# Weights 64 bytes (modulo 512) from their moving operands; the second FFN in 256-column matmuls; three output pieces summed on TensorE

## The chip, the core and the metric

One core of a Trainium2 chip runs the whole program. The time is device microseconds (us) of one execution; the kernel before has a median of 2463.41 us over three runs (2462.46 to 2465.11). Engines are named as in the profile: PE is TensorE's matmul side, PEld its weight loads, DVE VectorE, ACT ScalarE, POOL GpSimd, SP the engine that issues most DMAs.

## What is computed

Two layers of a decoder trunk over 256 positions of width 2048, in float32. Each layer adds three sub-layers to the residual stream: a token mixing (one input projection, three head groups, one output projection), a cross-attention into 256 memory tokens, and a SwiGLU FFN with 5632 hidden columns.

```python
def swiglu(h, w_gu, w_down):
    gu = jnp.einsum('bsd,dcf->bscf', h, w_gu)
    return jnp.einsum('bsf,fd->bsd', jax.nn.silu(gu[:, :, 0]) * gu[:, :, 1], w_down)

h = x
for l in range(DEPTH):                      # 2
    ...                                     # mixing and cross-attention, each h = h + rms_norm(.., g)
    ff = swiglu(rms_norm(h, f_pre_g[l]), f_w_gu[l], f_w_down[l])
    h = h + rms_norm(ff, f_post_g[l])
return h
```

## The kernel before

**The split.** A float32 product is made of three matmuls of the rounded type float32r. Each weight block (`raw`, 1 MB, loaded by SP) is split into `hi` (ACT, L208) and `lo` (DVE, L209), 1024 columns at a time, in rings of three buffers (pool `ws`). Activations exist as two halves too: `x` (normalised residual, transposed; made by `new_x`, L549), `mh`/`ml` (memory), `cqh`/`cql`, `kvn` (latents), `mxx` and `m6` (mixing result), `cx` (cross-attention result), `hx` (FFN hidden). All matmuls are recorded at the line of the helper `mm`, L203, so they are told apart by tiles: in `acc<-x,hi` the result is `acc`, and `x` and `hi` are the two operands. Each matmul has a weight load of its own (128 columns, 512 bytes of each partition), which PEld does beside the matmul ahead of it.

**Three forms of a projection.** `mm_t` (L394) puts the weights of the network into the array and moves `x`: for each 128x128 block three matmuls of 256 columns, lo by xh, hi by xh, hi by xl. `mm_w` (L413) does the same block with two: hi by both halves of `x` side by side (512 columns) and lo by xh (256 columns); the two halves of the result are added behind by `add_up` (L424: per tile one ACT copy and one DVE add out of PSUM). `mm_n` (L431) puts the activations into the array and moves hi, lo, hi, 256 to 512 columns each.

**Which form where.** Mixing, cross-attention queries and keys use `mm_t`; values and all output projections (`project_out`, L668) use `mm_n`. In both FFNs the first two steps of the up-projection (`hf == 0 and j < 4`) use `mm_t` and the other twenty use `mm_w`, two calls each: 40 calls of 16 blocks by 2, that is 1280 pairs of a 512- and a 256-column matmul in each layer. `plan` (L264) lists the weight blocks in the same order: for `mm_t` in the FFN one block of gate and up columns side by side (`pairs`, two DMAs of 512 KB per `raw`), for `mm_w` one 1 MB DMA.

**Addresses.** Pools lay tiles out one behind the other. `new_x` allocates 72 spare words and starts `x` `off` bytes ahead of them; `off` is 32 for mixing and cross-attention, 256 and 128 for the two FFNs. `pa` and `pc` hold 32 bytes each and shift what lies behind them. The distance used below is the address of the weights less that of the moving operand in the same partition, modulo 512 bytes, worked out from the places that the pools give the tiles. The strides of both are multiples of 512 bytes (but for the 336-column block of `ckv`), so a stage has one distance.

**Between stages.** After an output projection, `residual` (L611) adds the normalised result to `H` in pieces, and `turn_x` transposes and splits each into the next `x`; the first matmuls of the next stage follow piece by piece (the ramp). In two places `warm` (L444) gives PE 38 filler matmuls. Helper work of the attention runs as generators, advanced by `pump` once per weight block. At the end `last_residual` (L709) forms the statistics, then scales and adds eight pieces of 128x512: six on DVE (L721), two by ACT (scale, L718) and POOL (add, L719), each followed by its DMA out. A scheduler orders each engine's queue; in the ramps the order of DVE and ACT is that of the code.

## Time and profile before

| what | value |
|---|---|
| median of three runs | 2463.41 us |
| the profiled execution | 2460.3 us |
| its span, first to last instruction | 2458.6 us |
| PE busy | 2419.2 us, 98% |
| DVE, ACT, POOL busy | 59%, 50%, 12% |
| up-projection of the first FFN | about 484 to 737 and 859 to 1105 us |
| up-projection of the second FFN | about 1700 to 1955 and 2076 to 2323 us |

A matmul's recorded duration includes its pipeline, so neighbours overlap; what a matmul costs is the distance from its start to the next one's start. That is read from two rows of the timeline with the number of matmuls between them, from a piece of the chain of waits (`x168` is its count), or from a stretch that holds one form alone.

### The profile page before, as it was taken

How to read it: one execution, taken by the hardware profiler on the slowest of the kernel's cores; microseconds unless marked ns; L12 is line 12 of the kernel's file. 1: busy time of each engine (PE TensorE's matmuls, PEld its weight loads, DVE VectorE, ACT ScalarE, POOL GpSimd, SP SyncE). 2: the span in 40 equal slices, each digit the busy share in tenths (PEclk: the TensorE clock that was granted, in tenths of full speed). 3: DMA queues.
4: the chain of work that ended last, by engine and by line, in shares of the span. 5: the costliest groups of instructions: out<-in, count | busy, mean ns of one | idle time of the engine just before them, and what ended most of it. 6: DMA issues, size and time to landing. Idle time of an engine off the chain costs nothing.

```text
span 2458.6 us, 37634 instructions
## 1 busy us (share of the span) xinstructions
PE 2419.2 (98%) x15169; PEld 2170.7 (88%) x15169; DVE 1456.6 (59%) x2249; ACT 1240.9 (50%) x1936; POOL 296.8 (12%) x228
## 2 busy tenths in 40 slices
PE   9999999999999999999999999999999999999997
PEld 8899789998888988888999987998988889888887
DVE  5676767665554455555466767676555544555554
ACT  5655545564444444444455555465544444444443
POOL 0010131011110011111110102111111100111101
PEclk9999999999999999999999999999999999999999
DMA  7755575455555555555554555644555555555553
GB/s 247 238 168 155 165 259 176 154 172 188 188 189 191 186 193 188 188 186 197 180 171 131 190 147 194 206 171 150 181 188 187 188 195 189 186 187 187 188 194 129
DMA packets 362371, 452.95 MB, mean 184 GB/s; under 512 B 8730, under 2 KB 281044, under 8 KB 361684
## 3 DMA queue, kind: packets, MB, share of 16 engines
q1 hardware_dynamic: 360756, 443.97, 54.9%
q0 software_dynamic: 1248, 6.29, 0.8%
q8 instruction: 119, 1.95, 0.3%
q14 instruction: 56, 0.46, 0.1%
q10 hardware_dynamic: 192, 0.28, 0.0%
HBM read 444.72 MB, written 5.79 MB: 183 GB/s over the span
## 4 chain that ended last, share of the span: by engine, by line
PE 93%; DVE 3%; DMA 1%; ACT 1%; issue 0%; SPq 0%; DVEq 0%; ACTq 0%
PE acc L203 89%; DVE lo L209 1%; PE ixp L203 1%; PE xtp L595 1%; PE lga L203 0%; DVE mx L209 0%; ACT hi L208 0%; DVE H L624 0%; DMA H<-in_x_dram 0%; PE warm L448 0%; PE pva L203 0%; DMA m<-in_mem_dram 0%; PE pvb L203 0%; PE lgx L203 0%; PE pvx L203 0%
## 5 line engine op out<-in xcount | busy, mean ns | idle before, releaser
L209 DVE TENSOR_TENSOR lo<-raw,hi 128x1024 fp32r<-128x1024 f32 (+2 forms) x839 | 1012.9, 1208 | 813.5 <-ACT hi L208 812.4
L208 ACT ACTIVATE hi<-raw 128x1024 fp32r<-128x1024 f32 (+2 forms) x839 | 859.4, 1025 | 897.4 <-PE acc L203 812.9
L203 PE MATMUL acc<-x,hi 128*128 128x512 f32 (+2 forms) x4800 | 1298.7, 342 | 0.0
L203 PE MATMUL acc<-x,lo 128*128 128x256 f32 x3680 | 990.7, 282 | 7.9 <-ACT x L214 4.5
L203 PEld LDWEIGHTS acc<-x,hi 128*128 128x128 f32 (+1 forms) x4800 | 818.6, 188 | 107.7 <-issue 2.0
L203 PEld LDWEIGHTS acc<-x,lo 128*128 128x128 f32 x3680 | 691.6, 188 | 23.0 <-ACT x L214 9.7
L203 PE MATMUL acc<-hi,hx 128*128 128x512 f32 (+1 forms) x1760 | 452.6, 347 | 0.0
L203 PEld LDWEIGHTS acc<-hi,hx 128*128 128x128 f32 x1760 | 308.6, 189 | 41.7
L203 PE MATMUL acc<-lo,hx 128*128 128x512 f32 (+1 forms) x880 | 304.5, 347 | 0.0
L203 PEld LDWEIGHTS acc<-lo,hx 128*128 128x128 f32 x880 | 166.7, 189 | 20.3
L1272 POOL TENSOR_TENSOR u<-u,rbh 128x512 f32<-128x512 f32 x40 | 51.9, 1297 | 1004.0 <-DVE u L429 1004.0
L203 PE MATMUL acc<-hi,mx 128*128 128x512 f32 (+1 forms) x576 | 149.7, 347 | 7.1 <-ACT mx L208 5.3
L203 PEld LDWEIGHTS acc<-hi,mx 128*128 128x128 f32 x576 | 100.7, 191 | 21.3 <-ACT mx L208 6.3
L203 PE MATMUL acc<-hi,x 128*128 128x384 f32 (+1 forms) x384 | 110.0, 362 | 0.0
L1247 POOL TENSOR_TENSOR g<-g,u 128x512 f32<-128x512 f32 x44 | 92.6, 2104 | 72.0 <-ACT g L1257 68.9
L203 PE MATMUL acc<-lo,mx 128*128 128x512 f32 (+1 forms) x288 | 99.3, 345 | 0.0
L203 PEld LDWEIGHTS acc<-hi,x 128*128 128x128 f32 x384 | 70.0, 188 | 7.5 <-issue 2.0
L203 PE MATMUL acc<-lo,x 128*128 128x384 f32 (+1 forms) x192 | 69.3, 361 | 0.0
L214 ACT ACTIVATE x<-xtp,gT 128x256 fp32r<-128x256 f32 x96 | 40.2, 471 | 45.3 <-PE xtp L595 45.3
L427 ACT ACTIVATE g<-acc 128x256 f32<-128x256 f32 x80 | 30.5, 381 | 60.1 <-PE acc L203 60.1
L203 PEld LDWEIGHTS acc<-lo,mx 128*128 128x128 f32 x288 | 55.0, 191 | 6.2
L427 ACT ACTIVATE u<-acc 128x256 f32<-128x256 f32 x80 | 30.4, 379 | 58.5 <-PE acc L203 58.5
(250 smaller groups left out, 2053.2 us busy)
## 6 DMA issues: line engine op xcount, KB each, us to landing
raw<-in_f_w_gu_dram SPq DMA_DIRECT2D x160, 1024.0 KB, 5.0
raw<-in_f_w_down_dram SPq DMA_DIRECT2D x76, 1024.0 KB, 5.0
raw<-in_w_out_dram SPq DMA_DIRECT2D x30, 1024.0 KB, 5.3
raw<-in_w_in_dram SPq DMA_DIRECT2D x48, 512.0 KB, 4.8
raw<-in_w_in_dram SPq DMA_DIRECT2D x23, 1024.0 KB, 5.6
raw<-in_x_wkv_dram SPq DMA_DIRECT2D x16, 1024.0 KB, 4.9
raw<-in_f_w_gu_dram SPq DMA_DIRECT2D x32, 512.0 KB, 4.5
raw<-in_w_in_dram SPq DMA_DIRECT2D x12, 960.0 KB, 5.2
```

Source lines behind the costliest of these rows:

```text
L203: return nc.tensor.matmul(o, lhsT=lhsT, rhs=rhs, start=start, stop=stop, skip_group_check=True)
L208: nc.scalar.activation(hi, src, AF.Copy)
L209: eng.tensor_tensor(lo, src, hi.bitcast(F32), op=ALU.subtract)
L214: nc.scalar.activation(hi, src, AF.Copy, scale=scale)
L427: nc.scalar.activation(dst[:, b, :], t[:, 256:512], AF.Copy)
L595: nc.tensor.transpose(p[:, t * P:(t + 1) * P], src[:, t, (c + j) * P:(c + j + 1) * P], ident)
L1247: nc.gpsimd.tensor_tensor(g, g, u, op=ALU.mult)
L1272: nc.gpsimd.tensor_tensor(u, u, two(fnx["rb"]), op=ALU.mult)
```

## The change

**Distances.** `pa` is gone, `new_x` has 16 spare words, all `off` are 64, gaps of 384 bytes are put at the start of the pools `mp` and `kp`, and `cx` starts 128 bytes later. What results (bytes modulo 512; counts over both layers):

| moving operand, weights | columns, count | before | after |
|---|---|---|---|
| x, hi/lo: mixing, cross queries | 256, 2448 | 32 | 64 |
| x, hi/lo: odd blocks of ckv | 256, 144 | 352 | 384 |
| cqh/cql/kvn, hi/lo: latents | 256, 408 | 448 | 64 |
| mh/ml, hi/lo: memory keys | 256, 384 | 448 | 64 |
| hi/lo, mh/ml: memory values | 256, 384 | 64 | 448 |
| hi/lo, x: values of A, gating | 384, 384 and 512, 192 | 480 | 448 |
| hi/lo, kvn: values of B | 384, 48 | 64 | 448 |
| hi/lo, m6: part of the first piece of w_out | 512, 48 in each layer | 64; 192 | 448; 64 |
| hi/lo, mx and hx: w_out, f_w_down | 256 and 512 | 0 | 0 |
| hi/lo, cx: x_wo | 512, 144 and 256, 96 | 64 | 64 |
| x, hi/lo: first FFN, first two steps | 256, 384 | 256 | 64 |
| x, hi/lo: first FFN, the rest | 512 and 256, 1280 pairs | 256 | 64 |
| x, hi/lo: second FFN, first two steps | 256, 384 | 128 | 64 |
| x, hi/lo: second FFN, the rest | 1280 pairs, after: 3840 of 256 | 128 | 64 |

**Form.** In the second layer (`l` is 1) every step of the up-projection uses `mm_t` and `act` in place of `mm_w` and `act_w`, and `plan` loads its blocks as `pairs`.

**End.** In `last_residual` three of the eight pieces are summed in PSUM: PE adds `ident` by H, and, once the statistics are there, `dg` (the row factors on a diagonal, from `spread`) by `og`; ACT copies the sum out and issues its DMA. The other five stay on DVE. POOL has no part in it.

```diff
-    pa = ctx.enter_context(tc.tile_pool(name="pa", bufs=1))
-    nc.gpsimd.memset(pa.tile([P, 8], F32, name="half_pa"), 0.0)
...
-                    if hf == 0 and j < 4:
-                        yield spec(pairs(a["f_w_gu"][l], j * P, 256), KD, 512)
+                    if l or hf == 0 and j < 4:
+                        yield spec(pairs(a["f_w_gu"][l], (hf * nh + j) * P, 256), KD, 512)
...
-        x = xp.tile([P, f + 72], F32R, tag="xx", name=nm)[:, 72 - off // 4:72 - off // 4 + f]
+        x = xp.tile([P, f + 16], F32R, tag="xx", name=nm)[:, 16 - off // 4:16 - off // 4 + f]
...
+        pieces = [(t, slice(g * 512, (g + 1) * 512)) for g in range(4) for t in range(2)]
+        summed = {}
+        for t, f in pieces[:3]:
+            summed[t, f.start] = p = acc.tile([P, 512], F32, tag="acc", name="hsum")
+            mm(p, ident, H[:, t, f], True, False)
+        dg = spread(r)
         rest()
-        for t in range(2):
-            for c0, n, beside in ((512, 512, True), (0, 512, False), (1024, 512, False), (1536, 512, False)):
-                f = slice(c0, c0 + n)
-                if beside:
-                    nc.scalar.activation(og[:, t, f], og[:, t, f], AF.Copy, scale=r[:, t:t + 1])
-                    nc.gpsimd.tensor_tensor(H[:, t, f], H[:, t, f], og[:, t, f], op=ALU.add)
-                else:
-                    nc.vector.scalar_tensor_tensor(H[:, t, f], og[:, t, f], r[:, t:t + 1], H[:, t, f],
-                                                   op0=ALU.mult, op1=ALU.add)
-                (nc.scalar if t and beside else nc.sync).dma_start(out[0, t * P:(t + 1) * P, f], H[:, t, f])
+        for t, f in pieces[:3]:
+            mm(summed[t, f.start], dg[:, t, :], og[:, t, f], False, True)
+        for i in (3, 0, 4, 1, 5, 2, 6, 7):
+            t, f = pieces[i]
+            p = summed.get((t, f.start))
+            if p is not None:
+                nc.scalar.activation(H[:, t, f], p, AF.Copy)
+            else:
+                nc.vector.scalar_tensor_tensor(H[:, t, f], og[:, t, f], r[:, t:t + 1], H[:, t, f],
+                                               op0=ALU.mult, op1=ALU.add)
+            (nc.sync if p is None else nc.scalar).dma_start(out[0, t * P:(t + 1) * P, f], H[:, t, f])
...
-        res["x"] = xh, xl, _ = new_x("x", 32)
+        res["x"] = xh, xl, _ = new_x("x", 64)
...
+        nc.gpsimd.memset(mp.tile([P, 96], F32, name="gap"), 0.0)
...
+            nc.gpsimd.memset(kp.tile([P, 96], F32, name="gap"), 0.0)
...
-        begin(residual(og, oss, evac, ("x_pre_g", l), nx, False, 32), 2, -1)
+        begin(residual(og, oss, evac, ("x_pre_g", l), nx, False, 64), 2, -1)
...
-        cx = kp.tile([P, 2, 4, 256], F32R, name="cx")
+        cx = kp.tile([P, 2080], F32R, name="cx")[:, 32:].rearrange("p (a h t) -> p a h t", a=2, h=4)
...
-        begin(residual(og, oss, evac, ("f_pre_g", l), nx, True, (256, 128)[l]), 3, 0)
+        begin(residual(og, oss, evac, ("f_pre_g", l), nx, True, 64), 3, 0)
...
-                if hf == 0 and j < 4:
+                if l or hf == 0 and j < 4:
...
-            begin(residual(og, oss, evac, ("mix_pre_g", l + 1), cur, True, 32), 3, 0)
+            begin(residual(og, oss, evac, ("mix_pre_g", l + 1), cur, True, 64), 3, 0)
```

The queue of PE where the second half of the second FFN's up-projection starts, behind the last matmul of the down-projection, before (the number behind a name tells one tile from another; two `acc` tiles hold two blocks of 128 gate columns):

```order
L203 MATMUL acc_19895<-hi_19980,hx_16862 128x256
L203 MATMUL acc_20061<-x_16817,hi_20010 128x512
L203 MATMUL acc_20062<-x_16817,hi_20010 128x512
L203 MATMUL acc_20061<-x_16817,lo_20011 128x256
L203 MATMUL acc_20062<-x_16817,lo_20011 128x256
```

and with the change (the two tiles hold two blocks of gate and two of up columns):

```order
L201 MATMUL acc_20590<-x_16820,lo_20539 128x256
L201 MATMUL acc_20590<-x_16820,hi_20538 128x256
...
L201 MATMUL acc_20591<-x_16820,lo_20539 128x256
L201 MATMUL acc_20591<-x_16820,hi_20538 128x256
...
L201 MATMUL acc_20590<-x_16820,hi_20538 128x256 x2
L201 MATMUL acc_20591<-x_16820,hi_20538 128x256 x2
```

Two matmuls per block of weights became three, each of 256 columns and each with a weight load; outside this up-projection and the end PE's, DVE's and ACT's queues hold the same operations in the same order as before.

The queue of PE from the start of the last piece of the last output projection (132 matmuls, of which the middle is left out), before:

```order
L203 MATMUL acc<-hi,hx 128x256 [waits Activation_49]
L203 MATMUL acc<-hi,hx 128x256
L203 MATMUL acc<-lo,hx 128x256 [waits DVE_49]
...
L203 MATMUL acc<-hi,hx 128x256
L1318 UNCONDITIONAL_BRANCH
```

and with the change:

```order
L201 MATMUL acc<-hi,hx 128x256 [waits Activation_49]
L201 MATMUL acc<-hi,hx 128x256
L201 MATMUL hsum<-H,ident 128x512 [waits DVE_49]
L201 MATMUL acc<-lo,hx 128x256 [waits DVE_49]
...
L201 MATMUL acc<-hi,hx 128x256
L201 MATMUL hsum<-H,ident 128x512
L201 MATMUL hsum<-H,ident 128x512 [waits DVE_49]
L201 MATMUL hsum<-og,dg 128x512 [waits DVE_49,Pool_49]
L201 MATMUL hsum<-og,dg 128x512 [waits Pool_49]
L201 MATMUL hsum<-og,dg 128x512 [waits Activation_49]
```

One of the three sums of `H` stands ahead of the last piece's matmuls and waits for DVE to empty an `acc` tile of the piece before (L686 in the kernel before); the other two stand behind the last piece, and the three of `og` at the end.

The end of ACT's queue, before:

```order
L582 ACTIVATE sqj,sso<-og 128x256 [waits DVE_49,Activation_49] x2
L718 ACTIVATE og<-og,rs_r 128x512 [waits DVE_49,Pool_49]
L718 ACTIVATE og<-og,rs_r 128x512 [waits Pool_49]
L723 DMA out_dram<-H 128x512 [waits Pool_49]
L1318 UNCONDITIONAL_BRANCH
```

and with the change:

```order
L580 ACTIVATE sqj,sso<-og 128x256 [waits DVE_49,Activation_49] x2
L518 ACTIVATE dg<-ident,rs_r 128x128 [waits DVE_49]
L724 ACTIVATE H<-hsum 128x512 [waits PE_49]
L728 DMA out_dram<-H 128x512 [waits Activation_49]
L724 ACTIVATE H<-hsum 128x512 [waits PE_49] x2
L728 DMA out_dram<-H 128x512 [waits Activation_49] x2
L1325 UNCONDITIONAL_BRANCH
```

ACT now waits for PE where it scaled for POOL, and issues three DMAs where it issued one.

## Rows read from the trace of the kernel before

**Rows 1.** Page, part 1: busy time, share of the span, instructions.
```profile
PE 2419.2 (98%) x15169; PEld 2170.7 (88%) x15169; DVE 1456.6 (59%) x2249; ACT 1240.9 (50%) x1936; POOL 296.8 (12%) x228
```
**Rows 2.** Waits of PE: who for whom, total us, times, longest.
```profile
PE acc L203 <- DVE lo L209: 5.8, 8, 1.2
PE acc L203 <- ACT mx L208: 5.3, 4, 2.0
```
**Rows 3.** Stretches, PE alone: us, length, PE busy (matmuls), granted clock, DMA share, GB/s.
```profile
826.90:858.60 31.70, 31.70 (x266) 1.00 0.60 192
858.60:1104.80 246.20, 246.20 (x1410) 1.00 0.57 188
2076.00:2323.00 247.00, 247.00 (x1410) 1.00 0.57 188
```
**Rows 4.** Timeline of PE, cross-attention's output projection: start us, us, instruction.
```profile
458.72 0.40 PE L203 MATMUL acc<-lo,cx 128*128 128x512 f32 x1
...
472.02 0.39 PE L203 MATMUL acc<-hi,cx 128*128 128x512 f32 x1
472.38 0.28 PE L203 MATMUL acc<-lo,cx 128*128 128x256 f32 x1
...
477.59 0.28 PE L203 MATMUL acc<-hi,cx 128*128 128x256 f32 x1
```
**Rows 5.** Timeline of PE: latents at 82 us, cross-attention's queries at 411 us.
```profile
82.58 0.28 PE L203 MATMUL acc<-cqh,lo 128*128 128x256 f32 x1
...
85.40 0.28 PE L203 MATMUL acc<-cqh,lo 128*128 128x256 f32 x1
...
411.09 0.28 PE L203 MATMUL acc<-x,lo 128*128 128x256 f32 x1
...
423.99 0.28 PE L203 MATMUL acc<-x,hi 128*128 128x256 f32 x1
```
**Rows 6.** Chain of waits: start us, us, what; cross logits, then both FFNs' first steps.
```profile
430.44 0.86 PE lgx L203 x4
506.57 17.27 PE acc L203 x144
1723.63 17.08 PE acc L203 x144
```
**Rows 7.** Stretches: length, PE, PEld, DVE, ACT, POOL busy, granted clock, DMA, GB/s.
```profile
158.00:240.00 82.00, 81.71 (x633) 76.58 (x631) 55.01 (x140) 47.54 (x107) 4.64 (x5) 1.00 0.55 171
378.00:402.00 24.00, 22.79 (x195) 22.61 (x194) 22.58 (x40) 19.34 (x41) 6.96 (x4) 1.00 0.41 145
2445.00:2459.00 14.00, 0.00 (x0) 0.00 (x0) 8.53 (x19) 2.22 (x6) 4.83 (x4) 0.62 0.41 150
```
**Rows 8.** Groups of the second FFN (1742 to 2445 us): busy us, mean ns, idle before.
```profile
L209 DVE TENSOR_TENSOR lo<-raw,hi 128x1024 fp32r<-128x1024 f32 x248 | 308.1, 1242 | 290.2 <-ACT hi L208 290.2
L429 DVE TENSOR_TENSOR g<-acc,g 128x256 f32<-128x256 f32 x40 | 16.9, 421 | 13.6 <-ACT g L427 13.6
L1289 ACT ACTIVATE og<-acc 128x512 f32<-128x512 f32 x6 | 3.5, 588 | 2.9 <-PE acc L203 2.9
L1256 DVE TENSOR_TENSOR g<-acc,rbh 128x512 f32<-128x512 f32 x2 | 1.4, 688 | 0.2 <-PE acc L203 0.2
```
**Rows 9.** DMA issues: count, KB of each, median us to landing.
```profile
raw<-in_f_w_gu_dram SPq DMA_DIRECT2D x32, 512.0 KB, 4.5
```
**Rows 10.** Timeline of DVE at the last output piece and at the end.
```profile
2428.50 0.42 DVE L686 TENSOR_TENSOR og<-acc,og 128x256 f32<-128x256 f32 x1 [1.64 <-PE acc L203]
...
2448.43 0.16 DVE L505 SCALAR_TENSOR_TENSOR rs_r<-rs_u,rs_r 128x2 f32<-128x2 f32 x1
2448.71 6.08 DVE L721 SCALAR_TENSOR_TENSOR H<-og,rs_r,H 128x512 f32<-128x512 f32 x6
```
**Rows 11.** Single lines and tiles: count, ns min/median/max, first and last start.
```profile
L721 DVE SCALAR_TENSOR_TENSOR H<-og,rs_r,H x6: 740/749/1751, 2448.7 to 2454.0; 128x512 f32<-128x512 f32 x6
L519 DVE TENSOR_SCALAR dg<-ident,rs_r x10: 279/287/289, 27.1 to 1737.7; 128x128 f32<-128x128 f32 x10
```

## The prediction

> **What bounds the kernel now.** I read the page first: PE is busy for 98% of the span [rows 1]. Then the waits of PE: the longest sums are 5.8 and 5.3 us [rows 2], so nearly all of the 2460.3 us of the profiled execution is the spacing of matmuls. The question is what a matmul costs, and the rows to look at are starts, not durations. Granted clock is 1.00 (2.4 GHz) in the stretches used.
>
> Spacing of 256-column matmuls, by distance of weights from moving operand: at 0 bytes 31.70 us / 264 = 120.1 ns (the 266 of the row hold two that reach in from the side) [rows 3]; at 64, (477.59 - 472.38) / 46 = 113.3 ns, and 512 columns beside it (472.02 - 458.72) / 57 = 233.3 ns [rows 4]; at 448, (85.40 - 82.58) / 24 = 117.5; at 32, (423.99 - 411.09) / 109 = 118.3 [rows 5]; at 256, 17.27 / 144 = 119.9, and at 128, 17.08 / 144 = 118.6 [rows 6]. A pair of `mm_w` (512 and 256 columns) takes 246.20 / 704 = 349.7 ns at 256 and 247.00 / 704 = 350.9 at 128 [rows 3]. The reader is to see that one instruction of one shape costs 113 to 120 ns depending on the stage, that the stages differ in the distance, and that at 64 two matmuls of 256 columns (226.6) cost less than one of 512 (233.3). The one confounder: 64 is shown only by the form `mm_n`; `mm_t` is shown at 32, 128, 256 and 448. `mm_n` at 0 costs 120.1, though, so its form alone does not make 113.
>
> Here a rule speaks against the change. The Trainium skill ("SBUF — State Buffer", Who interferes with whom) gives PE two independent read ports, one for the moving operand and one for weight loads, and says "PE and ACT never wait on anyone"; by it a distance changes nothing. The trace disagrees: `hx` and `cx` are the same form at 120.1 and 113.3 ns. The Trainium skill's page "TensorE: Matmul & The Clock Gate" (Back-to-back issue gap) adds a fixed 2.5 ns to each matmul's columns, an estimate of 109.2 and 215.8 ns, by which three matmuls cost 2.6 ns more per block than the pair (3.3 us over 1280); at 64 the rows show the opposite sign.
>
> **The change, part by part.**
>
> *Second FFN, 1280 pairs become 3840 matmuls of 256 columns at 64.* A pair of 350.9 becomes 3 x 113.3 = 339.9: 11.0 ns x 1280 = **14.1 us gained**. PE alone sets the end in this stage (247.00 busy of 247.00 us [rows 3]), and must go on doing so. One split feeds 8 blocks, 8 x 339.9 = 2.72 us of PE, and takes DVE 1.24 us [rows 8]. The evacuation gets lighter: per step two DVE operations out of PSUM of 0.69 us in place of four of 0.42 and one in SBUF [rows 8], no ACT copies, one POOL multiply fewer. The loads come as two DMAs of 512 KB, 4.5 us each to land [rows 9]; a block lasts PE 5.4 us with three buffers, so even one after the other (9 us) they keep ahead.
>
> *First FFN, 1280 pairs from 256 to 64.* No row shows the mixed pair at 64. If both keep what they cost alone: 233.3 + 113.3 = 346.6 against 349.7, **4.0 gained**. Ends: 233.3 + 120.1 = 353.4 loses 4.7; as cheap as three of 256 (339.9) gains 12.5. I take the sum, as both addends are rows at this very distance.
>
> *First two steps of both FFNs.* Of 384 matmuls in each layer, those in the ramp follow the turning of x and gain nothing; I count the 144 of [rows 6] and the 120 behind them: 264 x (6.6 + 5.3) = **3.1 gained**, ends 0 and 4.6.
>
> *Mixing and cross queries, 2448 from 32 to 64.* 118.3 to 113.3; less 120 in each of the two mixing ramps: 2208 x 5.0 = **11.0 gained**. What could take it is a wait behind: DVE is 55 us busy in 82 us of mixing [rows 7], about two thirds, and `lo` is already the longest waiter's releaser [rows 2]. Ends: half lost (5.5) and all counted (12.2).
>
> *Latents, 408 from 448 to 64:* 4.2 ns each, **1.7 gained**, end 0 where they wait for their weights. *Memory keys and values swap:* the 384 of keys go 448 to 64, the 384 of values 64 to 448. Of the keys I count 72 a layer, since the others lie in a ramp in which DVE is 22.58 us busy of 24 [rows 7]: 0.6 gained against 1.6 lost, **1.0 lost**. *720 matmuls of 384 and 512 columns, mostly from 480 to 448:* no row; the spread over all distances of 256 columns is 6.8 ns, which would be 4.9 us either way. I take 0.
>
> *The gaps.* Small memsets on POOL, one ahead of the load of gX and of the memory's splits, one ahead of the residual adds; both wait for tiles that the instruction behind waited for before. Nothing.
>
> *The end.* Lost: the first sum of H stands in PE's queue ahead of 130 matmuls. It waits for DVE's emptying of an `acc` tile, done at 2428.92 [rows 10], some 0.3 us after PE gets there, and then costs two passes of 512 columns; four passes of 256 take 0.86 us [rows 6], so 0.86 again. All behind it is late by **1.2 us**. Gained: after the statistics (2448.6) DVE needs six operations, 6.08 us, since two took 1.75 us beside POOL's adds, the others 0.75 [rows 10, 11]. Now it needs 0.29 for `dg` [rows 11] and 5 x 0.75: done at about 2452.7 against 2454.8. The other path: three sums of 0.86 from 2449.0 end at 2451.6, a copy of 0.59 [rows 8] and ACT's DMAs follow, about 2452.7 too. So 2.1 gained, net **0.9**. In the last 14 us the clock averaged 0.62 [rows 7]: (1 - 0.62) / 0.5 x 14 = 10.6 us at 1.2 GHz, so it fell some 3.7 us after PE's last matmul. With the change PE stops at about 2446.3 and is needed at 2449.0, so I take full clock; at half clock the sums end 2.6 us later, the gain is gone and 1.2 to 1.7 are lost.
>
> **The sum.** 14.1 + 4.0 + 3.1 + 11.0 + 1.7 - 1.0 + 0.9 = 33.8 us off 2460.3, 2426.5. The median of the three runs stands 3.1 above the profiled execution; off 2463.4 the sum gives **2430 us**.
>
> **The rivals.**
>
> *Half the effect.* At 32 the spacing is a mean of unequal ones, and `mm_t` at 64 could settle at 116 instead of 113.3. Then 3.7 + 0.5 + 1.7 + 5.1 + 0.6 - 0.4 + 0.9 = 12.1: 2451. For it: no row shows `mm_t` at 64. Against: where both forms' stages can be compared (118 to 120 at all distances but 64), the form made little difference.
>
> *Slower: the 113 belongs to `mm_n`, not to 64.* Then the new three of the second FFN cost 3 x 118.5 to 3 x 120.1 = 355.5 to 360.3 against 350.9, 5.9 to 12.0 lost, everything else stays, the end gives 0.9: 2468 to 2475. It decides at 350.9 / 3 = 117.0 ns: above it the three matmuls lose. Against it stand `hx` and `cx`. The Trainium skill ("SBUF — State Buffer", Who interferes with whom), by its independent ports, would have the spacing unchanged as well; [rows 3, 4] do not bear it out.
>
> *It doesn't get its weights.* The halved loads of the second FFN arrive late and PE waits for `hi` and `lo`: 88 blocks, 1 us each, would make it 2430 + 88 = 2518. Against: 9 us for a pair, 16 us of cover.
>
> **How the numbers follow.** Forecast 0.80, half 0.10, slower form 0.07, weights 0.03. A measurement of this kernel can tell about 0.2%, 4.9 us. Forecast and half are faster (0.90); the slower form lies at the edge, 0.03 within and 0.04 beyond; with the weights 0.07 slower. The range takes the ends of the unknown terms: 8.5 more from the pairs and some 2 from the 384s gives 2419; pairs at their worst (8.7 less) and half of mixing lost (5.5) with 3 for the end and the 384s give 2447. Both together leave out the rivals, 0.2.
>
> **What would show it.** `acc<-x,hi` starts 113 to 114 ns apart in mixing and in the second FFN, whose second half is 239 us long, not 247; the first FFN's second half 244 us in place of 246; memory values at 117.5. In the waits of PE nothing above 10 us. At the end POOL idle and five scaled adds of 0.75 us. Wrong would be a spacing of `mm_t` above 117, unequal spacings that repeat, or DVE `lo` high among PE's releasers.

## The result, and the profile after

The changed kernel takes 2440.1 us (median of four runs, 2439.0 to 2442.9) against 2462.9 of the kernel before: a ratio of 0.9909, 95% interval 0.9892 to 0.9926. It is 22.8 us faster where 33.8 were forecast. The profiled execution took 2439.0 us, with a span of 2437.3 (2458.6 before), so the span lost 21.3 us. The shift of the stages' first matmuls between the two traces tells where:

| part of the span | gained, us | forecast, us |
|---|---|---|
| first layer up to its FFN | 1.7 | with the next but one: 11.7 |
| first FFN | -2.0 | 5.7 (pairs 4.0, first steps 1.7) |
| second layer up to its FFN | 6.1 | |
| second FFN | 15.5 | 15.5 (form 14.1, first steps 1.4) |
| the end | 0.0 | 0.9 |

The page of the changed kernel, part 1 (busy time, share, instructions), answers to [rows 1]; the three longest entries of PE's waits, and the one that is new, answer to [rows 2]:

```profile
PE 2402.6 (99%) x16461; PEld 2204.8 (90%) x16461; DVE 1432.9 (59%) x2189; ACT 1220.3 (50%) x1858; POOL 260.5 (11%) x209
```

```profile
PE acc L201 <- DVE lo L207: 7.8, 10, 1.5
PE acc L201 <- ACT mx L206: 5.5, 4, 2.0
PE acc L201 <- ACT x L212: 4.9, 10, 1.5
PE hsum L201 <- DVE dg L517: 2.7, 1, 2.7
```

PE is as full as before, and the only new wait of any size is 2.7 us at the end, for the row factors `dg`. The gain is spacing, that is, the time from one matmul's start to the next one's. Four stretches of the changed kernel (us, PE busy with its matmuls, PEld, DVE, ACT, POOL, granted clock, DMA share, GB/s): the second halves of the two FFNs' up-projections, as in [rows 3], and the middle of mixing in both layers, from its first to its last matmul with `x` moving.

```profile
857.05:1105.40 248.35, 248.35 (x1410) 215.85 (x1408) 139.10 (x152) 116.24 (x154) 34.65 (x20) 1.00 0.56 187
2062.35:2301.75 239.40, 239.40 (x2114) 239.40 (x2114) 127.81 (x119) 104.46 (x110) 17.61 (x10) 1.00 0.59 194
162.50:233.20 70.70, 70.70 (x582) 67.52 (x582) 47.10 (x124) 40.60 (x93) 4.16 (x4) 1.00 0.54 166
1379.50:1450.70 71.20, 71.20 (x582) 68.04 (x583) 47.49 (x127) 41.70 (x95) 3.27 (x4) 1.00 0.54 166
```

The same two stretches of mixing in the kernel before:

```profile
161.35:233.60 72.25, 72.25 (x582) 69.05 (x582) 47.16 (x124) 40.60 (x93) 4.16 (x4) 1.00 0.53 162
1381.10:1453.50 72.40, 72.40 (x582) 69.19 (x583) 47.59 (x129) 41.86 (x95) 3.27 (x4) 1.00 0.54 163
```

The second FFN's half now holds 2112 matmuls of 256 columns in 239.40 us, 113.4 ns each: three of them 340.1 ns, where a pair took 350.9 [rows 3]. The first FFN's half did not get shorter but longer: 248.35 / 704 = 352.8 ns a pair against 349.7. Mixing became 1.6 and 1.2 us shorter; 480 matmuls by 5.0 ns would have been 2.4 us in each layer.

The starts of PE's matmuls in second-layer mixing show why (timeline: start us, duration us, instruction). The first piece is one stretch between two interruptions by the attention, the second a later one:

```profile
1385.87 0.28 PE L201 MATMUL acc<-x,lo 128*128 128x256 f32 x1
...
1388.10 0.64 PE L201 MATMUL acc<-x,hi 128*128 128x256 f32 x4
...
1405.97 0.28 PE L201 MATMUL acc<-x,lo 128*128 128x256 f32 x1
...
1411.41 0.28 PE L201 MATMUL acc<-x,lo 128*128 128x256 f32 x1
```

From 1385.87 to 1388.10 lie 19 intervals, 117.4 ns each by these rounded starts (117.6 by the unrounded ones); from 1405.97 to 1411.41 lie 48, 113.3 each. Shape, operands and distance are the same. Interval by interval, each uninterrupted stretch of ten or more that lies at 64 throughout has one of two spacings, 117.8 (single intervals of 117 to 119) or 113.3 (113, 113, 114, repeated); below they are called slow and fast. A stretch takes its spacing within its first six matmuls and keeps it, for 23 matmuls or for 2111. Of the uninterrupted intervals of these two stretches of mixing 69% are of the fast kind in the first layer and 48% in the second.

### The profile page after: what moved, and what is told of

Its sections match the earlier page's. It is cut to its first block, busy times and chain, and to the rows that moved or that the text cites. A ratio compares the mean times of both kernels' runs of the same rounds, so it can differ in the third digit from the quotient of the medians.

```text
span 2437.3 us, 40157 instructions
## 1 busy us (share of the span) xinstructions
PE 2402.6 (99%) x16461; PEld 2204.8 (90%) x16461; DVE 1432.9 (59%) x2189; ACT 1220.3 (50%) x1858; POOL 260.5 (11%) x209
## 4 chain that ended last, share of the span: by engine, by line
PE 92%; DVE 4%; DMA 2%; ACT 1%; issue 1%; SPq 0%; POOL 0%; ACTq 0%; POOLq 0%; DVEq 0%
PE acc L201 87%; DVE lo L207 2%; PE ixp L201 1%; PE xtp L593 1%; DMA m<-in_mem_dram 1%; ACT hi L206 1%; PE lga L201 0%; DVE mx L207 0%; DVE H L622 0%; DMA H<-in_x_dram 0%; PE warm L446 0%; PE pvb L201 0%; PE pva L201 0%; PE lgx L201 0%; PE pvx L201 0%
## 5 line engine op out<-in xcount | busy, mean ns | idle before, releaser
L201 PE MATMUL acc<-x,hi 128*128 128x256 f32 (+2 forms) x6080 | 1282.0, 303 | 0.0
L201 PEld LDWEIGHTS acc<-x,hi 128*128 128x128 f32 (+1 forms) x6080 | 963.8, 188 | 57.1 <-issue 2.0
L201 PE MATMUL acc<-x,lo 128*128 128x256 f32 x3680 | 939.0, 280 | 9.0 <-ACT x L212 4.9
L1254 POOL TENSOR_TENSOR g<-g,u 128x512 f32<-128x512 f32 x44 | 84.5, 1921 | 589.2 <-ACT g L1264 587.6
L1279 POOL TENSOR_TENSOR u<-u,rbh 128x512 f32<-128x512 f32 x20 | 26.1, 1307 | 505.1 <-DVE u L427 505.1
L213 DVE SCALAR_TENSOR_TENSOR x<-xtp,gT,x 128x256 fp32r<-128x256 f32 x96 | 41.7, 475 | 18.9 <-ACT x L212 18.9
L201 PE MATMUL acc<-hi,cx 128*128 128x512 f32 (+1 forms) x160 | 42.8, 352 | 0.0
```

The lines of the kernel that those rows point to most:

```text
L201: return nc.tensor.matmul(o, lhsT=lhsT, rhs=rhs, start=start, stop=stop, skip_group_check=True)
L213: nc.vector.scalar_tensor_tensor(lo, src, scale, hi.bitcast(F32), op0=ALU.mult, op1=ALU.subtract)
L1254: nc.gpsimd.tensor_tensor(g, g, u, op=ALU.mult)
L1279: nc.gpsimd.tensor_tensor(u, u, two(fnx["rb"]), op=ALU.mult)
```

## Experiments

### The form without the distance, and the distance without the form

The kernel before, with one thing done (`ffn2_three_128`): the second FFN in matmuls of 256 columns, its `x` at 128.

```diff
-                    if hf == 0 and j < 4:
+                    if l or hf == 0 and j < 4:
...
-                if hf == 0 and j < 4:
+                if l or hf == 0 and j < 4:
```

Expected: 

> The kernel before with one thing done: the second FFN's up-projection in matmuls of 256 columns, its x still at distance 128. Theory (113 ns belongs to distance 64): 3 x 118.6 = 355.8 ns in place of a pair of 350.9, 1280 x 4.9 = 6.3 us slower than before, 2469 us. Rival (the form alone makes 113 ns in a long run without interruption, the distance nothing): 1280 x (350.9 - 339.9) = 14.1 us faster than before, 2449 us.

Measured: 2470.1 us, a ratio to the kernel before of 1.0032 (1.0021 to 1.0044): slower, by 7.8 us. Then the changed kernel with the second FFN back in pairs, at 64 (`ffn2_pairs_64`):

```diff
-                    if l or hf == 0 and j < 4:
+                    if hf == 0 and j < 4:
...
-                if l or hf == 0 and j < 4:
+                if hf == 0 and j < 4:
```

Expected: 

> The changed kernel with one thing undone: the second FFN's up-projection is back in pairs (512 and 256 columns), at distance 64. Theory (distance and form both needed): a pair costs at 64 what it costs in the first FFN of the changed kernel, 352.9 ns, against 3 x 113.3 = 339.9 for the three; 1280 x 13.0 = 16.6 us slower than the changed kernel, 2457 us. Rival 1 (the distance alone made the second FFN faster, the form nothing): about 2440. Rival 2 (the sum of my prediction, 233.3 + 113.3 = 346.6): 8.6 us slower than the changed kernel, 2449.

Measured: 2456.9 us, a ratio of 0.9976 (0.9966 to 0.9987), 16.8 us slower than the changed kernel. The second half of the second FFN's up-projection, first in `ffn2_three_128`, then in `ffn2_pairs_64` (columns as above):

```profile
2084.15:2334.85 250.70, 250.70 (x2115) 250.70 (x2114) 127.97 (x120) 104.28 (x110) 17.58 (x10) 1.00 0.58 185
```

```profile
2069.80:2318.20 248.40, 248.40 (x1410) 215.96 (x1409) 139.27 (x152) 116.33 (x154) 34.63 (x20) 1.00 0.57 187
```

At 128 the three cost 3 x 118.7 = 356.1 ns, at 64 a pair costs 248.40 / 704 = 352.8. Each edit alone makes this stage longer than the pair at 128 (350.9); together they make it 340.1. The two are one edit. It also settles the rival that gave the 113 to the form `mm_n`: the 2112 matmuls of `ffn2_three_128` and of the changed kernel are the same instructions in the same order, and 250.70 and 239.40 us differ by the addresses alone. Nor is it the place of one operand alone: `hi` and `lo`, moving from the same places, cost 120.1 ns with `hx` as weights and 113.3 with `cx` in the kernel before; and as weights in the same places they go with 118.7 ns here and 113.4 in the changed kernel, by the place of `x`. The Trainium skill ("SBUF — State Buffer", Who interferes with whom) has PE wait on nobody, with a read port each for moving data and weights; taken to cover PE's own two streams, it would have the two stages take the same time, and the measurement decides against that for these operands.

### The first FFN in the same form

`ffn1_three_64` is the changed kernel with the condition gone, so that both FFNs use `mm_t` throughout:

```diff
-                    if l or hf == 0 and j < 4:
+                    if True:
...
-                if l or hf == 0 and j < 4:
+                if True:
```

Expected: 

> The changed kernel with the first FFN in matmuls of 256 columns too, at 64. Theory: the pair of 352.9 ns becomes 3 x 113.3 = 339.9, 1280 x 13.0 = 16.6 us faster than the changed kernel, 2423 us. Rival (of the two spacings that the changed kernel shows at 64, 113.3 and 117.7 ns, this stage falls into the slow one and stays there): 3 x 117.7 = 353.1, no difference, 2440 us; with one of the two halves in it, 2432.

Measured: 2423.3 us, a ratio of 0.9846 (0.9830 to 0.9861). Its second halves in the first and the second layer:

```profile
849.70:1089.10 239.40, 239.40 (x2114) 239.40 (x2113) 127.86 (x120) 104.41 (x110) 17.60 (x10) 1.00 0.60 194
2047.70:2287.10 239.40, 239.40 (x2115) 239.40 (x2114) 127.87 (x120) 104.37 (x110) 17.59 (x10) 1.00 0.60 194
```

Both run at 113.4 ns throughout. The term for the first FFN's pairs, 4.0 gained, was not only of the wrong size; the place held 16.8 more for the form that the second FFN already had.

### Other distances

The sweeps keep the instructions and place `x` elsewhere, by `off` and a longer spare in `new_x` (the two gaps in `mp` and `kp` are left out to make room, which also sends the latents and memory keys to 448). The second sweep has all FFN steps in `mm_t`.

```diff
-        x = xp.tile([P, f + 16], F32R, tag="xx", name=nm)[:, 16 - off // 4:16 - off // 4 + f]
+        x = xp.tile([P, f + 112], F32R, tag="xx", name=nm)[:, 112 - off // 4:112 - off // 4 + f]
...
-        begin(residual(og, oss, evac, ("f_pre_g", l), nx, True, 64), 3, 0)
+        begin(residual(og, oss, evac, ("f_pre_g", l), nx, True, (32, 96)[l]), 3, 0)
```

Expected of `sweep_a`: 

> The changed kernel with other distances of the weights from x: first mixing 96, second mixing 80, cross queries 48 and 192, first FFN (pairs) 32, second FFN (three matmuls) 96; latents and memory keys go to 448, the output projection of cross-attention to 320. Read by spacing, stage by stage. Theory (64 is the only one of these with a fast spacing): 118 to 120 ns in all stages of 256 columns; the second FFN at 96 costs 4224 x 5.2 = 22 us more than the changed kernel, mixing and cross queries some 7 us, in all about 2469 us. Rival (a zone around 64 is fast): 113.3 ns at 48, 80 and 96 too, and perhaps no second spacing there; about 2437 us. The pair at 32 is open: between 346.6 and 352.9 ns.

Expected of `sweep_b`: 

> All FFN steps in matmuls of 256 columns, and x at other distances: first mixing 192, second mixing 448, cross queries 320 and 160, first FFN 192, second FFN 448. Theory A (with x moving, 113.3 ns belongs to 64 alone): 117.5 to 120 ns in all of these; both FFNs cost 8448 x 4.5 = 38 us more than with 64 everywhere, mixing and cross queries some 6 us, about 2467 us. Theory B (192 is fast too, as the output projection of cross-attention at 192 in the first sweep, 113.4 ns, would have it): first FFN 113 ns, second 117.7 at 448; about 2445 us.

The one run of `sweep_b` took 6258.5 us, with all stages some 2.5 times as long, and tells nothing of the distances; the same kernel ran again. Expected of `sweep_b_again`: 

> The kernel of sweep_b once more, whose only run was 2.5 times as long in all stages alike, at a recorded clock of 1.00 (on 512 columns 620 ns, 227 in all other runs), and told nothing of the distances. The expectations are those of sweep_b: 2467 us if 113.3 belongs to 64 alone (with x moving), 2445 if 192 is fast too.

Measured: `sweep_a` 2469.4 us (one run), `sweep_b_again` 2467.0, a ratio of 1.0021 (1.0009 to 1.0033). In `sweep_a` the second halves of the second FFN at 96 and of the first FFN in pairs at 32:

```profile
2084.25:2332.10 247.85, 247.85 (x2115) 247.85 (x2114) 127.92 (x119) 104.38 (x110) 17.63 (x10) 1.00 0.58 187
863.00:1111.50 248.50, 248.50 (x1411) 215.95 (x1410) 139.24 (x152) 116.39 (x154) 34.52 (x20) 1.00 0.58 187
```

In `sweep_b_again` the second halves of the first FFN at 192 and of the second at 448:

```profile
858.45:1107.20 248.75, 248.75 (x2115) 248.75 (x2114) 127.92 (x119) 104.19 (x110) 17.61 (x10) 1.00 0.58 187
2077.80:2326.50 248.70, 248.70 (x2114) 248.70 (x2113) 127.86 (x119) 104.14 (x110) 17.61 (x10) 1.00 0.58 187
```

With `x` moving the 256-column spacing is 119.2 ns at 48 and at 80, 117.4 at 96 (118.7 in some stretches), 119.9 at 160, and the pair at 32 takes 352.9. Pieces of the chain of waits (start us, us, what) show it: in `sweep_a` cross queries at 48 and mixing at 80,

```profile
405.89 7.87 PE acc L201 x66
1264.82 17.17 PE acc L201 x144
```

and in `sweep_b_again` mixing at 192 (the first row) and at 448:

```profile
31.60 19.06 PE acc L201 x168
1258.81 16.96 PE acc L201 x144
1408.95 7.15 PE acc L201 x63
```

So 16 bytes either side of 64 the gain is gone. But 64 is not alone. At 192, 320 and 448, which like 64 lie 64 beyond a multiple of 128, the same two spacings appear, and in the stretches at 0, 32, 48, 80, 96, 128, 160 and 256 no run of matmuls settles at 113.3. At 192 the 168 matmuls of the row ran at 113.5 ns, while 95% of the intervals in the later mixing and the whole FFN ran at 117.8; at 448 the 63 matmuls of the last row ran at 113.5, the 144 above them and the FFN at 117.8; at 320 the cross queries were 23.1 us long with 63% fast intervals, as at 64. Theory A of the second sweep thus held in its total and in the long stages, but not as it was worded: 113.3 does not belong to 64 alone, and 320 was not at 117.5 or more. One stage has to be named rightly: the pieces of cross-attention's output projection, which the expectation of `sweep_a` puts at 320, stand at 192 by the definition used here (weights less moving operand). They ran at 113.4 ns, at a distance at which `x` in the FFN stays at 117.8. What comes ahead of a stretch thus has a part in it, which the next runs take up.

### What an interruption does

`interrupted` is `ffn1_three_64` with transposes after every 24 matmuls of the FFN's up-projection, whose results nobody reads: two in the first layer's second half, one in the later steps of the second layer's first half, six in its second half.

```diff
+            if brk and n % 2:
+                p = ps2.tile([P, 512], F32, tag="lg", name="brk")
+                for _ in range(brk):
+                    tc.keep_in_program_order(nc.tensor.transpose(p[:, 0:P], H[:, 0, 0:P], ident))
```

Expected: 

> All FFN steps in matmuls of 256 columns at 64; work is added whose result nobody reads: after every 24 matmuls, 2 transposes of 128 columns in the second half of the first FFN's up-projection, 1 in the later steps of the second FFN's first half, 6 in its second half (776 in all, by some 109 ns 85 us). Read by the spacing of the 256-column matmuls between them. Theory (which of the two spacings a run of matmuls gets is drawn anew at every interruption): stretches of 24 at 117.7 and others at 113.3, as in mixing, mean 114.5 to 116; about 2520 us. Rival (the slow spacing in mixing comes from the other engines' work there, not from the interruption): 113.3 to 113.8 in nearly all; about 2512 us.

Measured: 2520.1 us (one run), the theory's total. But nothing is drawn. Behind a single transpose 54 of 71 stretches of 24 were slow, behind two 1 of 87, behind six none of 87, and the 54 are not scattered: three slow stretches and one fast one follow each other in this order over all 71. The starts of five single transposes show one round, 2.95, 2.93, 2.94 and then 2.86 us apart:

```profile
1754.86 0.27 PE L412 MATMUL brk<-ident,H 128*128 128x128 f32 x1
...
1757.81 0.27 PE L412 MATMUL brk<-ident,H 128*128 128x128 f32 x1
...
1760.74 0.27 PE L412 MATMUL brk<-ident,H 128*128 128x128 f32 x1
...
1763.68 0.27 PE L412 MATMUL brk<-ident,H 128*128 128x128 f32 x1
...
1766.54 0.27 PE L412 MATMUL brk<-ident,H 128*128 128x128 f32 x1
```

That the total was met is in part luck: the 55 slow stretches are 55 x 24 x 4.5 ns = 5.9 us of the 11.8 that remain of 2520.1 - 2423.3 us when the 85 of the transposes are taken off. A stretch behind one transpose and one ahead of a pair of them, in PE's timeline:

```profile
1851.24 0.27 PE L412 MATMUL brk<-ident,H 128*128 128x128 f32 x1
1851.27 0.36 PE L201 MATMUL acc<-x,lo 128*128 128x256 f32 x1
1851.47 0.28 PE L201 MATMUL acc<-x,hi 128*128 128x256 f32 x1
...
1853.12 0.28 PE L201 MATMUL acc<-x,hi 128*128 128x256 f32 x1
```

```profile
870.71 0.73 PE L201 MATMUL acc<-x,hi 128*128 128x256 f32 x5
...
872.07 0.74 PE L201 MATMUL acc<-x,hi 128*128 128x256 f32 x5
872.64 0.38 PE L412 MATMUL brk<-ident,H 128*128 128x128 f32 x2
```

The first has 14 intervals of 117.9 ns from 1851.47 to 1853.12, the second 12 of 113.3 from 870.71 to 872.07. The rival, that the other engines' work in mixing makes the slow spacing, is not needed: the other engines did the FFN's work here, the same in fast and in slow stretches. What is shown is that the interruption decides, and in a regular way; by what property, is open. In mixing, stretches behind groups of several transposes were slow too.

### The spacing is handed on

`all_three_out_192` was meant as a faster version: `ffn1_three_64` with `hi` and `lo` of the last two pieces of the output projections (256 columns, at 0, 120.0 ns) 320 bytes further in their buffers, so that the weights stand at 192; to fit, three blocks share a buffer instead of four.

```diff
-                hi = ws.tile([P, 1024], F32R, tag="hi", name="hi")
-                lo = ws.tile([P, 1024], F32R, tag="lo", name="lo")
+                o = 80 if sub == 3 else 0
+                hi = ws.tile([P, 1024], F32R, tag="hi", name="hi")[:, o:]
+                lo = ws.tile([P, 1024], F32R, tag="lo", name="lo")[:, o:]
...
-                    yield spec(rows(wd, c0, n), nh, n)
+                    yield spec(rows(wd, c0, n), nh, n, None, 3 if n == 256 else None)
```

Expected: 

> All FFN steps in matmuls of 256 columns at 64, and in the output projections of mixing and the FFNs the hi and lo of the 256-column pieces lie 320 bytes further in their buffers, three blocks to a buffer in place of four, so that weights stand 192 bytes from the moving operand in place of 0 there. Theory (the distance sets the spacing whichever operand moves): 1440 matmuls from 120.0 to 113.4 ns, 9.5 us less than with the FFNs alone, 2414 us. Rival 1 (0 costs 120.0 because of the form, not the distance): 2423 us. Rival 2 (the smaller splits, more of them, make PE wait for hi and lo in these pieces): above 2423 us.

Measured: 2439.4 us, a ratio of 0.9908 (0.9891 to 0.9924): 16 us slower than `ffn1_three_64`, and none of the three expectations gives the reason. The two pieces and the half of the up-projection behind them, first layer:

```profile
814.90:845.90 31.00, 31.00 (x265) 31.00 (x264) 14.38 (x16) 14.39 (x21) 0.00 (x0) 1.00 0.58 186
845.90:1094.65 248.75, 248.75 (x2114) 248.75 (x2114) 127.19 (x119) 104.32 (x110) 17.56 (x10) 1.00 0.58 188
```

The pieces run at 117.8 ns, and the half behind them, untouched and with PE never idle, went from 239.40 to 248.75: all its 2112 matmuls at 117.8. `hand_over` tests that the spacing is taken over. In the first layer both pieces stand at 64; in the second the one is at 192 and the other, which comes last, at 0.

```diff
+    SHIFT = ((112, 112), (80, 0))
...
-                    yield spec(rows(wd, c0, n), nh, n, None, 3 if n == 256 else None)
+                    yield spec(rows(wd, c0, n), nh, n, None, (3, SHIFT[l][c0 == 1792]) if n == 256 else None)
```

Expected: 

> All FFN steps in matmuls of 256 columns at 64, and the 256-column pieces of the output projections at other distances, three blocks to a buffer: in the first layer 64 for both pieces; in the second layer 192 for the one and 0 for the other, which comes last. Theory (a stage that follows without a pause takes over the spacing, and behind 0 bytes, 120.0 ns, comes the fast one): in the second layer the second half of the FFN's up-projection starts behind 0 bytes and is at 113.3 ns, 239 us, where it was 248.6 behind 192 bytes; in the first layer the two pieces at 64 decide: if they run at 113.4 the half behind them does too (239 us, 31.6 us of pieces become 30.0), if at 117.7 it takes that over (249 us). In all 2421 us in the first case, 2430 in the second. Rival (the slow halves behind 192 bytes came from the smaller buffers or from chance): no such rule, the second layer's half again at 248 us.

Measured: 2433.5 us (two runs), a ratio of 0.9880 (0.9851 to 0.9908), the second of the two cases, some 3 us above its 2430. The pieces and the half of the first layer; the last piece and the half of the second:

```profile
817.70:848.75 31.05, 31.05 (x265) 31.05 (x264) 14.40 (x16) 14.44 (x21) 0.00 (x0) 1.00 0.59 187
```

```profile
848.75:1097.45 248.70, 248.70 (x2114) 248.70 (x2113) 127.13 (x119) 104.28 (x110) 17.56 (x10) 1.00 0.58 188
2039.50:2055.35 15.85, 15.85 (x134) 15.85 (x133) 7.31 (x8) 7.39 (x11) 0.00 (x0) 1.00 0.60 192
2055.35:2294.70 239.35, 239.35 (x2114) 239.35 (x2113) 127.05 (x119) 104.38 (x110) 17.60 (x10) 1.00 0.60 195
```

Behind pieces at 117.8 the half runs at 117.8; behind a piece at 0 (120.0) it runs at 113.3, with the same small buffers. The pieces at 64 are slow behind 512 columns at 0, where those of cross-attention at 64, behind 512 columns at 64, run at 113.6. The rule that fits the uninterrupted places of these kernels: at 64 a run is fast behind 120.0 ns and behind 113.3, slow behind 117.8 and behind 512 columns at 0. It was found from these runs, and it holds for 64 only: in `sweep_b_again` the FFNs' second halves at 192 and 448 were slow directly behind 120.0.

### Using the rule

`take_over` leaves the first buffer of the pieces (18 matmuls) at 0 and puts the rest at 64, in mixing and FFN.

```diff
+                o = 0 if at_0 is None or at_0 and k0 + j == 0 else 112
...
+                    yield spec(rows(wd, c0, n), nh, n, None, (3, c0 == 1536) if n == 256 else None)
```

Expected: 

> All FFN steps in matmuls of 256 columns at 64; in each output projection of mixing and FFN the first buffer of the 256-column pieces (18 matmuls) stays at 0 and the rest of both pieces lies at 64, three blocks to a buffer. Theory (a run takes over the fast spacing behind 0 bytes, 120.0 ns, and the slow one behind 512 columns at 0): the 246 matmuls of the FFN's pieces and the 174 of mixing's run at 113.3, and what follows without a pause (x of the FFN's second half, memory keys) at 113.3 as well; 4 x 246 + 2 x 174 = 1332 matmuls x 6.7 = 8.9 us less than the 2423.3 us with the FFNs alone, 2414.5 us. Rival (with hi and lo moving, 64 behind 0 is slow as in the kernel with 64 in both pieces): 117.8 ns in the pieces and in the half behind them, about 2439 us.

Measured: 2419.7 us, a ratio of 0.9830 (0.9814 to 0.9847). The spacings came out as forecast: the 246 matmuls of the first layer's FFN pieces at 64, and the half behind them:

```profile
820.00:847.90 27.90, 27.90 (x249) 27.90 (x248) 13.68 (x15) 13.26 (x18) 0.00 (x0) 1.00 0.64 204
847.90:1087.20 239.30, 239.30 (x2114) 239.30 (x2113) 127.18 (x119) 104.34 (x110) 17.60 (x10) 1.00 0.60 196
```

Of the 8.9 us only 3.6 arrived. The stage behind mixing's pieces, memory keys with the ramp of the next `x`, first in `take_over`, then in `ffn1_three_64`, first layer:

```profile
370.50:400.10 29.60, 26.83 (x221) 26.66 (x221) 25.48 (x48) 21.06 (x45) 6.67 (x5) 0.94 0.46 160
```

```profile
373.10:399.90 26.80, 25.33 (x221) 25.15 (x221) 24.50 (x48) 21.15 (x45) 7.62 (x5) 1.00 0.51 168
```

It is 2.8 us longer (1.1 in the second layer), with 1.5 us more of PE at work and 1.3 more of PE idle: PE waits 2.8 us at once for `lo` there, 1.5 in `ffn1_three_64`, and the granted clock averages 0.94, which is (1 - 0.94) / 0.5 x 29.6 = 3.6 us at half clock and would account for the 1.5 (an estimate from this row). DVE is 24.5 to 25.5 us busy in this stage, so a PE that comes early finds it busy; this reason is argued, not tested. `take_over_ffn` leaves mixing's pieces as in the changed kernel.

```diff
-                yield spec(rows(w_out, c0, n), KD, n, MIX_FIRST if i == 0 else None, (3, c0 == 1536) if n == 256 else None)
+                yield spec(rows(w_out, c0, n), KD, n, MIX_FIRST if i == 0 else None)
```

Expected: 

> As take_over, but the output projection of mixing as in the changed kernel (256-column pieces at 0, four blocks to a buffer). Theory (in take_over the FFN's pieces kept their gain, and mixing's lost theirs and more to the stage of memory keys behind them, where PE waited for DVE and the step lasted 29.6 and 28.1 us in place of 26.8 and 27.0): 4 x 246 matmuls x 6.7 = 6.6 us less than the 2423.3 us with the FFNs alone, 2416.7 us. Rival (the gain was lost elsewhere, in the FFN or in the smaller buffers): mixing's pieces are missing from the gain, 2422 us.

Measured: 2418.2 us (2417.0 to 2419.3), a ratio of 0.9825 (0.9809 to 0.9841), the fastest of all: 5.1 us less than `ffn1_three_64`, where 6.6 were expected. Against `take_over` its median is 1.4 us lower, but both profiles have a span of 2417.3, so it is not settled that mixing's pieces cost anything; they bring nothing. Of the missing 1.5 us the traces show 0.9: three of the FFN's four pairs of pieces became 1.6 us shorter (29.9 us in place of 31.6 from first to last start), the last, at the end of the kernel, only 0.7 (from 32.63 to 31.91, counted from the last 512-column matmul).

### The end

`old_end` is the changed kernel with the eight scaled adds of before.

```diff
-        for t, f in pieces[:3]:
-            mm(summed[t, f.start], dg[:, t, :], og[:, t, f], False, True)
...
+                if beside:
+                    nc.scalar.activation(og[:, t, f], og[:, t, f], AF.Copy, scale=r[:, t:t + 1])
+                    nc.gpsimd.tensor_tensor(H[:, t, f], H[:, t, f], og[:, t, f], op=ALU.add)
```

Expected: 

> The changed kernel with the end of before. By my sum the new end gains 0.9 us (1.2 lost for the first sum in the queue of PE, 2.1 gained behind): the last piece of the last output projection 31.6 us long in place of 32.4, and from its last matmul to the end of the span about 1.7 to 2.1 us more than in the changed kernel. Rival (no gain behind, since the three sums or ACT's copies end as late as DVE's six): the end behind the last matmul is no longer than in the changed kernel, and the changed end loses 0.8.

Measured: 2440.4 us (one run), too close to tell by the time. By the trace the way from the last 512-column matmul to the last one of 256 is 31.78 us, and 32.63 in the changed kernel; from there to the end of the span 13.89 and 13.33. The new end gains 0.56 behind the last matmul and loses 0.85 ahead of it. The 0.3 between them is no more than the scatter: behind the last matmul the traces of the other kernels with the new end have 13.1 to 13.4 us, once 14.0, and those with the old end 13.9 to 14.2. In the changed kernel's chain and in DVE's and ACT's timeline it reads:

```profile
2428.64 4.26 PE hsum L201 x6
```

```profile
2428.41 3.40 DVE L726 SCALAR_TENSOR_TENSOR H<-og,rs_r,H 128x512 f32<-128x512 f32 x5
```

```profile
2432.92 0.60 ACT L724 ACTIVATE H<-hsum 128x512 f32<-128x512 f32 x1 [1.11 <-PE hsum L201]
```

And in stretches (columns as above):

```profile
2426.00:2428.60 2.60, 0.00 (x0) 0.00 (x0) 2.29 (x13) 0.39 (x1) 0.43 (x1) 1.00 0.00 0
...
2428.60:2429.40 0.80, 0.76 (x2) 0.49 (x3) 0.80 (x2) 0.01 (x1) 0.00 (x0) 1.00 0.00 0
2429.40:2430.20 0.80, 0.80 (x3) 0.27 (x2) 0.80 (x2) 0.42 (x1) 0.00 (x0) 0.80 0.17 67
2430.20:2431.00 0.80, 0.80 (x3) 0.28 (x2) 0.80 (x2) 0.17 (x1) 0.00 (x0) 0.50 1.03 387
```

DVE is done at 2431.81, 1.7 us ahead of the end of ACT's last copy. PE's three sums take 4.26 us, 1.42 each where 0.86 were counted: PE has been idle for 2.7 us when they start, and in the second of them the granted clock goes from 1.00 to 0.50 (from 2.4 to 1.2 GHz). The last copy starts at 2432.92, and its DMA is the last to be issued.

## Why the prediction was right, and where it was not

- **The second FFN, 14.1 us and 1.4 for its first steps.** Right in mechanism and size: 15.5. Both halves run at 113.4 ns, PE alone sets the end (239.40 busy of 239.40), and the halved loads keep up. The two single edits show that this needs both form and distance.
- **The first FFN's pairs, 4.0 gained.** Wrong in sign: 1280 x (352.8 - 349.7) = 4.0 lost. The step that failed is the sum 233.3 + 113.3, each taken from a stage of its own kind. Inside the pair the 256-column matmul takes 118 ns and the 512-column one 235. The lower end of the bounds, 4.7 lost, was nearly met. In the first half 576 of the pairs lost 1.8 us and the first steps gained 1.6 of the 1.7 that were counted: it is as long as before (253.7 and 253.8). The second half is 2.2 longer.
- **Mixing and cross queries, 11.0 gained.** Right in sign, but half the size: the eight stretches with `x` at 64 became 5.4 us shorter in sum, ramps included. The factor 5.0 supposed one spacing at 64. `cx` had shown only the fast one, in a stage that follows 512 columns at 64; stretches that the attention interrupts have either. The check: 480 x (0.69 x 5.0 + 0.31 x 0.5) = 1.7 us for the first layer against 1.6 measured, and with 0.48 and 0.52 1.3 against 1.2 for the second. This is the rival of half the effect, in this term alone and by another mechanism: not 116 everywhere but two values. The trace of the kernel before already held the slow one at 64, in one short stretch of the memory values in each layer; in the first it is this piece of the chain of waits, 1.77 us / 15 = 118 ns:

```profile
442.98 1.77 PE acc L203 x15
```

- **Latents, 1.7 gained; memory values, 1.6 lost.** Those of `cqh`/`cql` became 0.7 us longer in the first layer and 0.3 shorter in the second, those of `kvn` 0.1 shorter in each: the gain is not there, at a mean of 115.9 ns at 64, with waits among them. Memory keys became 0.5 shorter in sum and memory values 0.4 longer, 0.1 gained where keys and values together were counted as 1.0 lost. The values at 448 ran at 115.4, not the 117.5 that was named as a sign: 53% of their uninterrupted intervals were fast and the rest slow, as at 64.
- **384 and 512 columns, 0.** Five of the six stages became shorter by 0.1 to 0.5 us each and one longer by 0.2; 1.2 in sum, inside the bounds of 4.9.
- **The end, 0.9 gained.** Nothing against before in the profiled executions, and 0.3 lost against the old end in the same kernel. The 1.2 for the first sum was 0.85; behind, 2.1 became 0.56 (0.8 against the kernel before), because the sums ran at half clock for the most part. The text had named that case with its price and taken full clock.
- **The rivals.** That 113 belongs to `mm_n` is refuted by `ffn2_three_128` against the changed kernel; the weights were not late (7.8 us is PE's longest sum of waits for `lo`).
- **The signs of being wrong.** Two of them came in part: a spacing of `mm_t` above 117, in 31% of the first layer's mixing and 52% of the second's, and `lo` as the longest of PE's releasers, at 7.8 us where it was 5.8.

Together: 8.0 us of the pairs, 5.6 of mixing and cross queries, 1.8 of the latents and 0.9 of the end are missing. On top came 1.1 from the memory's keys and values, 1.2 from the 384 and 512 columns and 1.4 by which the 512-column pieces of `w_out` were shorter: 0.3 longer in the first layer, and in the second 1.7 shorter (60.4 in place of 62.1 us; 60.4 to 63.2 in the other kernels). That is 12.6 us; between the forecast of 33.8 and the 21.3 that the span lost lie 12.5. Most of the 1.7, 7 x 0.2 us, is the clock and not the distances: in the kernel before seven of those matmuls start 0.43 us apart at a granted clock of 0.52, behind a wait of 2.0 us for `mx`, and with the same wait the changed kernel stays at 1.00 (PE alone, columns as in [rows 3]; before, then after):

```profile
1526.80:1530.20 3.40, 3.40 (x9) 0.52 0.99 404
1502.20:1562.90 60.70, 57.10 (x257) 1.00 0.72 235
```

The time fell into the range because the largest term was right. The 3.7 us on top came from terms that had been put at nothing or at a loss; that they covered part of what was missing is luck.

## What to carry to other kernels

Where PE is full, look at the interval from start to start, stage by stage, and at the addresses of both operands: 256-column matmuls of one shape took 113.3 to 120.1 ns here, and the fastest version is 1.75% faster than the kernel before with the same multiplications. Measure a form at the distance where it will stand, never as a sum of its parts: the pair is the better form at 128 and the three at 64. Test a distance in every kind of stage that will have it: 64 had shown 113.3 in the one stage that was read, and has 117.8 as well. And look at how a stage is entered: a change to the 31 us ahead of it cost a stage of 240 us 9 us without touching it.

## What the runs showed of the hardware

- Two spacings of one matmul stream at one distance: 113.3 and 117.8 ns, kept for up to 2111 intervals; which one is set within the first six matmuls. They appear at 64, 192, 320 and 448 bytes, and no stretch at 0, 32, 48, 80, 96, 128, 160 or 256 settled at 113.3.
- The spacing passes from stage to stage without a pause: 120.0 ns at 0 bytes is followed by 113.3 at 64 (by 117.8 at 192 and 448), 117.8 by 117.8 at 64.
- Distance changes of 16 bytes matter: 119.2 ns at 48 and 80, 113.3 or 117.8 at 64.
- The 512-column spacing depends on it as well: 227 ns at 0, 229.0 at 192, 233.3 at 64.
- One transpose between stretches of 24 left 54 of 71 slow, three of every four in a fixed order; two left 1 of 87, six none of 87. Why is open, and so is what in the array or the memory makes the two spacings.
- The granted clock fell to one half while PE was at work again, after 2.7 us of idleness; in the kernel before it averaged 0.52 for 3.4 us behind a wait of 2.0, and behind the same wait the changed kernel stayed at 1.00.
